# Issuing the stores of a gated activation from GpSimd's software queue instead of the scalar queue

## The chip, the cores and the metric

One core of one Trainium2 chip. The metric is the device time of one execution in microseconds (us). A time quoted is the median of the runs of a kernel. A ratio is the mean time of one kernel's fast runs over the mean of the other's fast runs of the same rounds, so it is not quite the ratio of the medians.

## The reference

```python
x = randn(8192, 8192) as float32
a, b = np.split(x, 2, axis=-1)
return a * (1 / (1 + np.exp(-b)))        # out: 8192 x 4096
```

It reads 268.4 MB and writes 134.2 MB, and computes one sigmoid and one product per output.

## The kernel before

The rows go through in 32 tiles of 256 rows, two rows per partition. There are two slots for the input (64 KB per partition each) and two for the output (32 KB per partition each). SP loads, ACT computes the sigmoid in place, DVE multiplies into the output slot, and ACT issues the store:

```python
xs = [pool.tile([P, R * n_cols], fp32, name=f"x_sb{k}") for k in range(SLOTS)]   # SLOTS = 2, R = 2
os = [pool.tile([P, R * half], fp32, name=f"o_sb{k}") for k in range(SLOTS)]
...
load = nc.sync.dma_start(out=xs[i % SLOTS], in_=x_t[i])
...
def store(cols):
    ins = nc.scalar.dma_start(out=out_t[i, :, cols], in_=os[i % SLOTS][:, cols])
...
    sig = nc.scalar.activation(out=b, in_=b, func=SIG)
    mul = nc.vector.tensor_mul(out=packed[:, r, c], in0=rows[:, r, 0, c], in1=b)
    ...
    by_sigmoid = i % 2 == 1 and len(parts) == 1
    implied(mul, *(s for s in old["stores"] if by_sigmoid or s not in freed))
    if by_sigmoid:
        for s in freed:
            tc.add_manual_dep(sig.ins, s.ins.name, DEP, reason="frees the output slot")
```

`implied` declares that a dependency needs no wait of its own. `freed` holds the stores of the tile two before, which free the output slot. In every second tile the sigmoid waits for them, in the others the product does. The first and the last tile are computed in four pieces; the last tile is also stored in four.

## Time and profile before

| | before |
|---|---|
| time, median | 933.88 us (933.03 to 934.08, 3 runs) |
| busy DVE, ACT | 30%, 24% of the span |
| DMA, 103 to 914 us | 434 GB/s, share 1.00 |
| a tile | one sigmoid every 29.0 us |
| a product, a sigmoid of a whole tile | 8.69 us, 7.03 us |

The share of the DMA engines is the time in which their packets were under way, averaged over the 16. (The profile counts a packet whole where it starts, so a short stretch can read a little over 1.00, as 0 to 22 us does with 1.02.) At 1.00, as here from 103 to 914 us, there is no time left in which a faster issue could start anything earlier. What bounds this kernel is therefore not read from the chain of waits (it gives DVE 15%), but from two things together: the share, and the *reserves*, that is, how long before it is needed each transfer is queued or done. The lines are in the prediction.

### The profile page before, as it was taken

Reading aid. Unit: us, or ns where it says so; the run is one execution under the profiler, and the core shown is the slowest. Engines: PE = TensorE matmul, PEld = TensorE weight load, DVE = VectorE, ACT = ScalarE, POOL = GpSimd, SP = SyncE. Lnnn points to the kernel's source line nnn. Section 1 sums busy time; section 2 is a strip of 40 time slices with the busy share of each in tenths; the row PEclk is TensorE's granted clock in tenths of the full one; section 3 lists DMA queues with packets and bytes.
Section 4 is the critical chain, followed back from the end, with each engine's and each line's share of the span. In section 5 each row is a group of like instructions: output and inputs, shape, how many; then the busy total and the mean of one; then the engine's idle time right before and its main releaser. Section 6 shows DMA issues by size and latency. Waiting matters only on the chain.

```text
span 931.7 us, 247 instructions
## 1 busy us (share of the span) xinstructions
DVE 278.7 (30%) x38; ACT 227.1 (24%) x39; POOL 0.2 (0%) x4
## 2 busy tenths in 40 slices
DVE  0333213333133331233312333123331233312333
ACT  1323330233311333113331133311333113332033
POOL 0000000000000000000000000000000000000000
DMA  9999999999999999999999999999999999999999
GB/s 405 428 450 428 422 456 405 450 428 428 450 418 438 428 436 442 428 428 450 447 408 428 442 459 428 413 460 411 450 428 425 453 408 447 428 428 450 425 430 405
DMA packets 9649, 402.67 MB, mean 432 GB/s; under 512 B 1072, under 2 KB 1072, under 8 KB 1072
## 3 DMA queue, kind: packets, MB, share of 16 engines
q1 hardware_dynamic: 4608, 268.44, 66.6%
q10 hardware_dynamic: 5040, 134.22, 33.4%
q14 instruction: 1, 0.01, 0.0%
HBM read 268.44 MB, written 134.22 MB: 432 GB/s over the span
## 4 chain that ended last, share of the span: by engine, by line
DMA 73%; DVE 15%; ACT 12%; issue 0%; ACTq 0%
DMA x_sb<-in_x_dram 73%; DVE o_sb L69 15%; ACT x_sb L68 12%; ACTq L62 0%; ACTq L68 0%
## 5 line engine op out<-in xcount | busy, mean ns | idle before, releaser
L69 DVE TENSOR_TENSOR o_sb<-x_sb 128x8192 f32<-128x8192 f32 (+1 forms) x38 | 278.7, 7344 | 647.1 <-ACT x_sb L68 647.1
L68 ACT ACTIVATE x_sb<-x_sb 128x8192 f32<-128x8192 f32 (+1 forms) x38 | 225.8, 5952 | 695.6 <-DMA x_sb<-in_x_dram 694.4
L68 ACT ACT_TABLE_LOAD x1 | 1.3, 1283 | 0.8 <-PEq L188 0.8
L188 POOL MEMSET const-bfloat16-1.0<- 128x1 bf16 x1 | 0.1, 102 | 0.0
L188 POOL MEMSET const-uint8-127<- 128x1 uint8 x1 | 0.1, 102 | 0.0
L188 POOL MEMSET const-float32-0.0<- 128x1 f32 x1 | 0.1, 99 | 0.2 <-issue 0.2
L188 POOL MEMSET const-float32-1.0<- 128x1 f32 x1 | 0.1, 99 | 0.0
## 6 DMA issues: line engine op xcount, KB each, us to landing
out_dram<-o_sb ACTq DMA_DIRECT2D x31, 4096.0 KB, 34.7
out_dram<-o_sb ACTq DMA_DIRECT2D x4, 1024.0 KB, 5.6
x_sb<-in_x_dram SPq DMA_DIRECT2D x32, 42.2
```

The lines of the kernel that those rows point to most:

```text
L68: sig = nc.scalar.activation(out=b, in_=b, func=SIG)
L69: mul = nc.vector.tensor_mul(out=packed[:, r, c], in0=rows[:, r, 0, c], in1=b)
L188: nc = _bacc.Bacc("TRN2", target_bir_lowering=False, num_devices=1)
```

## The change

The intent: take the stores off ACT's stream, so that a sigmoid never stands behind a store that waits for its product (in the kernel before this held ACT once, for 0.94 us, in the last tile), and let GpSimd, which was busy for 0.2 us there, issue them. The wait for the output slot goes to the sigmoid in every third tile instead of every second. The last two pieces stay on the scalar queue, presumably to end sooner, and the call that keeps the sigmoids in program order goes.

```diff
-        def store(cols):
-            ins = nc.scalar.dma_start(out=out_t[i, :, cols], in_=os[i % SLOTS][:, cols])
-            now["stores"].append(ins)
-
-        chunks = []
         for k, (r, c) in enumerate(parts):
 ...
-            by_sigmoid = i % 2 == 1 and len(parts) == 1
+            by_sigmoid = i % 3 == 2 and len(parts) == 1
 ...
-            tc.keep_in_program_order(sig)
             now["sigs"].append(sig)
             now["muls"].append(mul)
-            chunks.append(slice(r.start * half + c.start, r.start * half + c.stop))
-            if i == n_tiles - 1 and k > 0:
-                store(chunks[k - 1])
-        store(chunks[-1] if i == n_tiles - 1 else slice(0, R * half))
+            if i == n_tiles - 1:
+                cols = slice(r.start * half + c.start, r.start * half + c.stop)
+                queue = nc.scalar if k >= len(parts) - 2 else nc.gpsimd
+                store = queue.dma_start(out=out_t[i, :, cols], in_=os[i % SLOTS][:, cols])
+                now["stores"].append(store)
+        if i < n_tiles - 1:
+            now["stores"].append(nc.gpsimd.dma_start(out=out_t[i], in_=os[i % SLOTS]))
```

## The prediction

> **What bounds the kernel now.** I read the page first for the busy shares and the transfer rate, then the table of stretches for the rate in the steady part, then the timeline of one tile, then the waits, and the tile view for how long transfers take. The page:
>
> ```profile
> span 931.7 us, 247 instructions
> DVE 278.7 (30%) x38; ACT 227.1 (24%) x39; POOL 0.2 (0%) x4
> DMA  9999999999999999999999999999999999999999
> DMA packets 9649, 402.67 MB, mean 432 GB/s; under 512 B 1072, under 2 KB 1072, under 8 KB 1072
> q1 hardware_dynamic: 4608, 268.44, 66.6%
> q10 hardware_dynamic: 5040, 134.22, 33.4%
> DMA 73%; DVE 15%; ACT 12%; issue 0%; ACTq 0%
> ```
>
> No compute engine is busy for more than 30% of the span, and the 16 DMA engines are busy in every slice. The two queue lines say how transfers are cut: q1 holds the 32 loads, 4608/32 = 144 packets each, which I read as 128 data packets (one per partition, 8 MB/128 = 64 KB) and 16 completions. q10 holds 31 + 4 stores, 5040/35 = 144 each, so 32 KB per data packet in the 31 large ones. Reads are twice the writes, and the queues split the engines 2 to 1.
>
> The stretches (start:end and length, then busy time of DVE, ACT and POOL, clock, DMA share, GB/s):
>
> ```profile
> 0.00:22.00 22.00, 0.00 (x0) 1.33 (x2) 0.20 (x4) 1.00 1.02 429
> 22.00:45.00 23.00, 8.90 (x4) 7.47 (x5) 0.00 (x0) 1.00 0.98 410
> 103.00:914.00 811.00, 243.38 (x28) 196.75 (x28) 0.00 (x0) 1.00 1.00 434
> 925.00:928.00 3.00, 0.80 (x1) 0.00 (x0) 0.00 (x0) 1.00 1.00 421
> 928.00:930.00 2.00, 0.00 (x0) 0.00 (x0) 0.00 (x0) 1.00 1.00 422
> 930.00:931.70 1.70, 0.00 (x0) 0.00 (x0) 0.00 (x0) 1.00 0.49 207
> ```
>
> From 103 to 914 us the DMA engines are never idle and move 434 GB/s. All bytes at this rate are 402.67/434 = 927.8 us. So only about 4 us of the 931.7 us are not pure transfer at full rate: the start, a thin place at 22 to 45 us, and the last 1.7 us. The chain of waits puts 27% on DVE and ACT, but it follows one of the two slots alone: load 42.2, sigmoid 7.0, product 8.7, together 57.9 us per two tiles, while the other slot's load lies beside the compute. 57.9/2 = 29.0 us per tile is what 12.58 MB need at 434 GB/s. Shorter compute would only lengthen the time from issue to landing.
>
> The timeline around one tile, and the tile view of the output tensor, give the reserves:
>
> ```profile
> 582.58 58.54 SPq L50 DMA_DIRECT2D x_sb<-in_x_dram  x3
> 582.58 0.36 ACTq L62 DMA_DIRECT2D out_dram<-o_sb  x1
> 596.01 7.03 ACT L68 ACTIVATE x_sb<-x_sb 128x8192 f32<-128x8192 f32 x1 [22.18 <-DMA x_sb<-in_x_dram]
> 625.01 7.03 ACT L68 ACTIVATE x_sb<-x_sb 128x8192 f32<-128x8192 f32 x1 [21.97 <-DMA x_sb<-in_x_dram]
> 632.07 8.69 DVE L69 TENSOR_TENSOR o_sb<-x_sb 128x8192 f32<-128x8192 f32 x1 [20.31 <-ACT x_sb L68]
> ...
> DMA to landing us min/median/max: 5.4/34.7/34.9
> ```
>
> At 582.58 a product has ended; the load into its slot and its store are issued together. The load before it lands only at 596.0, so the load queue has its next work 596.0 - 582.6 = 13.4 us early. The store lands at 582.6 + 34.7 = 617.3; the sigmoid two tiles later, where odd tiles wait for the slot, starts at 625.0 (7.7 us in reserve), and its product, where even tiles wait, at 632.1 (14.8 us in reserve). The waits agree: no wait of ACT or DVE is put down to a store.
>
> ```profile
> ACT x_sb L68 <- DMA x_sb<-in_x_dram: 694.4, 32, 22.3
> DVE o_sb L69 <- ACT x_sb L68: 647.1, 33, 23.9
> ```
>
> [...]
>
> **The change, part by part.**
> - 33 of the 35 stores leave ACT: 33 x 0.36 = 12 us of ACT queue time go. ACT idles 22 us before each tile, so nothing of it is on the path.
> - The same 33 are written by GpSimd. [...] It falls into the 7.7 us reserve of each store; the engines meanwhile work on the load that was queued 13.4 us or more before. 0 us on the path. DVE is idle for 20.3 us after each product[...].
> - The instruction order has 10 sigmoids (tiles 2, 5, ..., 29) and 20 products that wait for a store, where before had 14 and 16. The waits are met 7.7 or 14.8 us early: 0 us.
> - GpSimd also waits for the store eight before, since eight semaphores go round: 8 x 29 = 232 us old. 0 us.
> - The last tile: the third sigmoid no longer stands behind a store (0.94 us of idle ACT). DVE sets that chain: its products ran from 916.65 to 925.80, and four of 2.29 us need 9.16 of these 9.15 us. Gain at most 0.2 us. The last store is issued at 925.8 by ACT as before, 1 MB at 434 GB/s is 2.4 us, but it shares the engines with what is queued, and the engines are full until 930. The end is the drain of a backlog whose bytes are the same. [...]
> - [...]
> [...] What can't be read from before is whether the software queue moves the same bytes as efficiently; for this I add 1.5 us. 933.9 + 2 = about 936 us.
>
> **The rivals.**
> - Smaller descriptors. If GpSimd cuts 32 KB rows into pieces of some 4 KB, each piece costs a fixed part. [...] For it: nothing in before fixes the cut. Against: 32 KB contiguous per partition leaves no need.
> - [...]
> - Another split between queues. Now 64 KB and 32 KB packets seem to alternate and both queues progress in the ratio of their work. If the software queue gets a larger share, stores land earlier and loads still are queued ahead: 934. If it gets a smaller one, stores land after more than 42 us and ACT begins to wait for stores on every third tile, on DVE after 49 us; the engines would still have the late stores to do while loads are held, so most of this is hidden: 935 to 945.
> - Faster. The floor is 927.8 us of transfer plus the start and the receipt of the last write, so about 930 by the span: 0.3% at best. Over 2% isn't there.
>
> **Range and chances.** The structure holds the time at the transfer bound, so nearly all weight is within 2% (915.2 to 952.6 us). 8 in 10: 932 to 950, skewed up because each uncertain term costs and none pays. Slower by over 2%[...]: 0.14. Faster by over 2%: 0.01. The rest, 0.85, is within.
>
> **What would show it right or wrong.** Right: the steady stretch at 433 to 434 GB/s with DMA share 1.00, 144 packets per store in the new queue, sigmoids 29.0 us apart, no ACT or DVE wait on a store, stores landing some 34 to 36 us after issue. Smaller descriptors: several times 144 packets and a lower rate at share 1.00. [...] Another split: store landings far from 34.7 us, and ACT or DVE waits on stores if late. Wrong altogether: POOL busy for many us per store, so that stores start late and the DMA share has holes; or a tail after the last product that is much longer than 6 us.

The small terms came to under 1 us with them; of those only the gain of at most 0.2 us in the last tile is left. With the 1.5 us, an allowance that comes from no trace, the sum was given as 2 us on top of 933.9, hence about 936 us.

What the packet records of the kernel before show: of the 144 packets of a transfer 128 carry data and 16 are of 4 bytes. A data packet of 64 KB took 2.418 us, one of 32 KB 1.213 us and one of 8 KB 0.309 us (medians): 1.205 us for each further 32 KB, so a fixed part of about 0.008 us per packet. The last landing came 0.32 us after the end of the last data packet. The queues do alternate: from the first to the last of the 128 data packets of a store, 96 packets of loads started (29 of the 30 large stores after the first). And in the changed kernel eight semaphores go round on GpSimd's stores; by the order of the records the store issued at 235.3 us follows the wait for the first, issued at 33.0 us, which is seven back.

## The result

The changed kernel takes 934.25 us (933.54 to 934.53, 6 runs), before in the same rounds 933.55 us (933.03 to 934.15, 6 runs): ratio 1.0006, 95% interval 0.9993 to 1.0019. The time is the same.

From the page of the changed kernel (the group line has the count, then busy us and the mean in ns, then the idle time before it):

```profile
q0 software_dynamic: 4752, 132.12, 32.8%
q10 hardware_dynamic: 288, 2.10, 0.5%
L82 POOL DMA_DIRECT2D out_dram<-o_sb x31 | 16.6, 536 | 886.5 <-DVE o_sb L66 886.5
```

The new queue q0 holds 33 stores in 4752 packets, 144 each as in the hardware queue: the 32 KB rows stayed whole. Its share per byte is that of q10 before (32.8% for 132.12 MB against 33.4% for 134.22 MB). GpSimd's instruction for a store takes 0.53 us.

Two of the same stretches as before:

```profile
22.00:45.00 23.00, 8.90 (x4) 7.20 (x4) 0.67 (x1) 1.00 0.95 388
103.00:914.00 811.00, 243.38 (x28) 196.81 (x28) 14.88 (x28) 1.00 1.00 434
```

The steady part is the same to the last digit: 434 GB/s, share 1.00. The thin place at 22 to 45 us reads 388 GB/s against 410 before, which is some 1.2 us of this execution (23 us x (1 - 388/410)). It doesn't follow the queue: two later runs read 399 GB/s there with the hardware queue (E3) and 410 with the software queue (E4).

One tile in the timeline, the waits, and the time to landing in the tile view of the output tensor:

```profile
583.77 58.33 SPq L52 DMA_DIRECT2D x_sb<-in_x_dram  x3
584.04 0.53 POOL L82 DMA_DIRECT2D out_dram<-o_sb  x1 [28.38 <-DVE o_sb L66]
597.04 7.03 ACT L65 ACTIVATE x_sb<-x_sb 128x8192 f32<-128x8192 f32 x1 [22.02 <-DMA x_sb<-in_x_dram]
626.00 7.03 ACT L65 ACTIVATE x_sb<-x_sb 128x8192 f32<-128x8192 f32 x1 [21.92 <-DMA x_sb<-in_x_dram]
...
DMA to landing us min/median/max: 5.2/34.6/35.4
```

```profile
POOL out_dram L82 <- DVE o_sb L66: 886.5, 31, 32.6
ACT x_sb L65 <- DMA x_sb<-in_x_dram: 695.8, 32, 22.5
DVE o_sb L66 <- ACT x_sb L65: 648.3, 32, 23.8
```

The load is issued at once when the product ends; the store starts on GpSimd 0.27 us after the load, where ACT started it with the load. It lands 34.6 us later, at 618.6, and the sigmoid two tiles on starts at 626.0: 7.4 us of reserve remain, against 7.7 before. (In this tile the product carries the wait. For the tile before it, whose sigmoid does, the same sum gives 597.04 - 555.13 - 34.6 = 7.3 us.) Sigmoids are 29.0 us apart as before. No wait of ACT or DVE is put down to a store, and GpSimd itself waits for nothing but products.

### The profile page after: what moved, and what is told of

Its sections match the earlier page's. It is cut to its first block, busy times and chain, and to the rows that moved or that the text cites. A ratio compares the mean times of both kernels' runs of the same rounds, so it can differ in the third digit from the quotient of the medians.

```text
span 933.1 us, 258 instructions
## 1 busy us (share of the span) xinstructions
DVE 278.6 (30%) x38; ACT 226.8 (24%) x39; POOL 17.9 (2%) x37
## 2 busy tenths in 40 slices
DMA packets 9649, 402.67 MB, mean 432 GB/s; under 512 B 1072, under 2 KB 1072, under 8 KB 1072
## 3 DMA queue, kind: packets, MB, share of 16 engines
q0 software_dynamic: 4752, 132.12, 32.8%
HBM read 268.44 MB, written 134.22 MB: 432 GB/s over the span
## 4 chain that ended last, share of the span: by engine, by line
DMA 73%; DVE 15%; ACT 12%; DVEq 0%; issue 0%; ACTq 0%
DMA x_sb<-in_x_dram 73%; DVE o_sb L66 15%; ACT x_sb L65 12%; DVEq L170 0%; ACTq L65 0%
## 5 line engine op out<-in xcount | busy, mean ns | idle before, releaser
L82 POOL DMA_DIRECT2D out_dram<-o_sb x31 | 16.6, 536 | 886.5 <-DVE o_sb L66 886.5
L79 POOL DMA_DIRECT2D out_dram<-o_sb x2 | 1.1, 531 | 18.6 <-DVE o_sb L66 18.6
## 6 DMA issues: line engine op xcount, KB each, us to landing
out_dram<-o_sb POOLq DMA_DIRECT2D x31, 4096.0 KB, 34.6
x_sb<-in_x_dram SPq DMA_DIRECT2D x32, 42.2
```

What stands on the lines that cost most here:

```text
L79: store = queue.dma_start(out=out_t[i, :, cols], in_=os[i % SLOTS][:, cols])
L82: now["stores"].append(nc.gpsimd.dma_start(out=out_t[i], in_=os[i % SLOTS]))
```

## The experiments

Twelve kernels ran, all with correct results. The theory: the time is that of the transfers, both kernels have the same transfers, and everything the change touches lies within the reserves. If so, two kinds of test must show it. More work inside the reserves must cost nothing, and where the reserves are taken away, the differences between the two kernels must come out. The rivals: the software queue is just as fast in itself; or a gain by one part hides a loss by another.

### E12: one part alone, the waits

```diff
-            by_sigmoid = i % 2 == 1 and len(parts) == 1
+            by_sigmoid = i % 3 == 2 and len(parts) == 1
```

> The kernel before with nothing changed but the waits for the output slot: on the sigmoid in tiles 2, 5, ..., 29 instead of 3, 5, ..., 29. One part of the change alone. Theory (the waits are met 7.7 or 14.8 us before they are asked): ratio 0.999 to 1.001 to before. If the changed kernel were the sum of a gain by one part and a loss by another, this would show over 0.2% either way.

933.39 us against 933.24: ratio 1.0000 (0.9988 to 1.0013). The waits alone move nothing, so the change isn't a gain by the waits hidden by a loss by the rest, or the reverse, beyond the 0.1% or so that the interval leaves.

### E3 and E4: more DVE work inside the reserve, and a DVE copy that holds GpSimd up

After each large product two useless copies run on DVE, over the input slot that is no longer needed, once in the kernel before and once in the changed one:

```diff
             now["muls"].append(mul)
+            if len(parts) == 1:
+                for _ in range(2):
+                    junk = nc.vector.tensor_copy(out=b, in_=rows[:, r, 0, c])
+                    implied(junk, *old["sigs"], *old["muls"], *old["loads"], *now["loads"])
```

> The kernel before with two useless copies on DVE after each large product, written over the x slot (results stay right). If the copies take 4.3 us each DVE has 8.6 us more per tile, 258 us in all, and the next load into the slot is issued 8.6 us later: its queue reserve sinks from 13.4 to about 5 us. Theory (transfer bound, reserves cover it): within 0.3% of before, 931 to 937 us, though the chain of waits gave DVE 15% of the span. Rival (the chain of waits is right that DVE is on the path): 8.6 us per tile pair per slot, so up to 130 us more. Control for the next run.

> The changed kernel with the same two copies right after each product[...]. Lock theory[...]: the POOL instruction of a store takes 4 to 9 us instead of 0.53, the store lands that much later counted from the end of its product; the sigmoid's wait on every third tile had 7.7 us in reserve, so the time is 933 to 945 us. No-lock theory: POOL stays at 0.53 us, landing as before. In both, the same within 2%; if slower by over 2% the lock also eats the reserves.

E3 took 933.94 us (ratio 1.0004, interval 0.9989 to 1.0019), E4 933.89 us (1.0003, 0.9988 to 1.0018). DVE's busy time rose from 279 to 544 us and nothing followed: the 13.4 us in which loads were queued ahead took up all of it. So DVE's 15% in the chain of waits was no cost. That chain must call something the reason for each wait, even where a transfer would only have waited longer in its queue: the loads, issued later, landed 33.3 us after issue instead of 42.2 (medians).

The timeline of E4:

```profile
499.11 4.43 DVE L78 COPY x_sb<-x_sb 128x8192 f32<-128x8192 f32 x1
...
524.75 8.89 DVE L78 COPY x_sb<-x_sb 128x8192 f32<-128x8192 f32 x2
525.01 4.29 POOL L86 DMA_DIRECT2D out_dram<-o_sb  x1 [25.81 <-DVE o_sb L66]
```

The first line shows a single copy: 4.43 us. The pair at 524.75 has its first copy end near 529.18, and the POOL instruction ends at 529.30. GpSimd's instruction for a store, 0.53 us in the changed kernel, takes 4.29 us here (the median of the 31), until 0.12 us after the first copy; the second copy, which ran on to 533.64, held it no longer. So the lock theory is right in what it expects of the time: a copy on DVE held GpSimd's store instruction up. What ties the two no run shows. The stores landed 36.8 us after their issue, against 31.4 in E3; that was still in time. In the changed kernel as it stands, DVE idles when GpSimd issues the large stores (from 583.77, where a product ends and GpSimd's instruction follows at 584.04, to the next product). The product itself did not hold GpSimd up: its instructions for the first two stores of the last tile took 0.53 us each, at 920.54 and 922.75, while DVE was at the products of the next pieces (917.95 to 926.85).

### E1 and E2: the reserve taken away

One output slot instead of two, in the kernel before (E1) and the changed one (E2). Every product now waits for the store of the tile before it.

```diff
-    os = [pool.tile([P, R * half], fp32, name=f"o_sb{k}") for k in range(SLOTS)]
+    os = [pool.tile([P, R * half], fp32, name="o_sb0")] * SLOTS
```

(The lists of freed stores follow: each product waits for the last tile's store, the sigmoids for none.)

> The kernel before with one output slot instead of two, so that every product waits for the store of the tile before it and the time from the end of a product to the landing of its store comes onto the path. Theory (the store's path is hidden in both kernels by 7 to 15 us of reserve): with the reserve gone the engines run dry during each product; a tile takes one product (8.7 us) plus the landing of a store that shares the engines with one load (4.2 + 8.4 MB at 434 GB/s = 29 us, and about 2 us of issue and receipt), so some 39.5 us and 1250 to 1290 us in all. Rival (the output slots are not what holds things together, the transfer bound alone counts): stays within 2% of 934 us. This is the control for the next run.

> The changed kernel with one output slot. Theory that the software queue is slower per store but hidden in the changed kernel: POOL starts 0.29 us after the product where ACT starts 0.02 us after, and then takes 0.53 us against 0.36, so 0.3 to 0.8 us more per tile on the path, 31 tiles: 9 to 25 us (0.7 to 2%) slower than the same kernel with the hardware queue. Rival (nothing differs at all, the paths are equally fast): within 0.3% of it. Rival (the software queue delivers fewer bytes per us, hidden somewhere): more than 3% slower.

E1 took 1306.13 us (ratio to before 1.3996), a little over the range expected (a store took 32.7 us to land, not 31; the 2 us for issue and receipt were an estimate, and a store alone, in E11, took 11.1 us, of which 0.84 us pass before its first data packet and 9.7 are its bytes at 434 GB/s); E2 took 1298.06 us (1.3920). The first part of the expectation holds: without reserve the kernel is 40% slower and the DMA share from 103 to 800 us falls to 0.73. The second part is a miss: the software queue was not 9 to 25 us slower but 8 us *faster*, though GpSimd starts later, and none of the three expectations gave that. The difference is 0.6%, small, but the runs do not overlap (1305.06 to 1309.14 and 1297.21 to 1303.84 us, 4 each). The waits of DVE, E1 first:

```profile
DVE o_sb L70 <- DMA out_dram<-o_sb: 996.5, 31, 33.8
```

```profile
DVE o_sb L67 <- DMA out_dram<-o_sb: 988.9, 31, 34.3
```

(996.5 - 988.9)/31 = about 0.25 us less per tile between the end of a product and the landing of its store. So either the software path is faster in itself, or the sharing with the load beside it changed. E11 was made to tell these apart.

### E11: the disputed cost by itself

From the changed kernel: each load waits for the store of the tile before, so that nothing lies beside a store; stores of odd tiles go through GpSimd, those of even ones through ACT.

```diff
+        for s in last_stores[(i + 1) % SLOTS]:
+            tc.add_manual_dep(load.ins, s.ins.name, DEP, reason="nothing beside a store")
 ...
-            now["stores"].append(nc.gpsimd.dma_start(out=out_t[i], in_=os[i % SLOTS]))
+            now["stores"].append((nc.gpsimd if i % 2 else nc.scalar).dma_start(out=out_t[i], in_=os[i % SLOTS]))
```

> The disputed cost by itself: every load waits for the store of the tile before, so nothing lies beside a store, and stores of odd tiles go through GpSimd, those of even tiles through ACT, in one execution. A tile takes a load (8.4 MB, about 22 us as the first one took), 15.8 us of compute and a store (9.7 us at 434 GB/s and some 2 us more): about 49.5 us, 1560 to 1620 us in all. What counts is the time from the end of the product to the next load's issue, odd against even tiles. Theory of a slower software path: odd tiles 0.3 to 0.9 us longer. Theory after the one-slot runs (software landing is no later, though it starts later): within 0.2 us or shorter on odd tiles; then the gain there is in the path of the store itself, else it came from the sharing with a load.

1557.69 us in one run, just under the range expected. The chain of waits (start, length, what), first an even tile, then an odd one:

```profile
515.35 8.70 DVE o_sb L68
524.05 0.02 issue
524.07 11.10 DMA out_dram<-o_sb
535.17 0.02 SPq L52
...
564.26 8.70 DVE o_sb L68
572.97 0.28 issue
573.25 11.35 DMA out_dram<-o_sb
584.60 0.02 issue
```

From the end of the product to the landing: 535.17 - 524.05 = 11.12 us by ACT, 584.60 - 572.96 = 11.64 us by GpSimd. By itself the software path is 0.5 us slower per 4 MB store: 0.27 us until it starts and 0.25 us more to landing. Where these 0.25 us lie, the stretches right after the two issues show:

```profile
524.07:524.85 0.78, 0.00 (x0) 0.00 (x0) 0.00 (x0) 1.00 0.00 0
573.25:574.30 1.05, 0.00 (x0) 0.00 (x0) 0.53 (x1) 1.00 0.00 0
```

Nothing moves yet in either. By the packet records of the trace the first data packet starts 0.84 us after the issue by ACT (median of 16 stores, 0.84 to 0.88) and 1.10 us by GpSimd (15 stores, 1.09 to 1.23). From there to the landing both take 10.26 us, so once a store moves, the two queues are equally fast, though odd tiles also use the other output slot.

So the slower-path theory is right about the path, and the 0.25 us that E2 gained must have come where a store and a load share the engines. The packet records fit: the store's first data packet starts 6.9 us after its issue in E2 and 4.6 us in E1 (medians), so the two mix differently. Whether this is because the load's issue comes 0.27 us first in E2, or by another difference between the two kernels, is left open; no run varied the order by itself. In the changed kernel both effects are inside the 7.4 us of reserve and show nowhere.

### E5 to E8: small pieces, the prediction's first rival

Output slots with a gap of 16 bytes after every 4 KB (C = 1024), or after every 1 KB (C = 256), so that a store can't move whole rows. From the kernel before (the product and the last pieces are re-cut in the same way):

```diff
-    os = [pool.tile([P, R * half], fp32, name=f"o_sb{k}") for k in range(SLOTS)]
+    C = 1024
+    os = [pool.tile([P, R * half // C, C + 4], fp32, name=f"o_sb{k}") for k in range(SLOTS)]
 ...
+        cut = os[i % SLOTS][:, :, 0:C]
+        out_v = out_t[i].rearrange("p (q c) -> p q c", c=C)
 ...
-            ins = nc.scalar.dma_start(out=out_t[i, :, cols], in_=os[i % SLOTS][:, cols])
+            ins = nc.scalar.dma_start(out=out_v[:, cols], in_=cut[:, cols])
```

> The kernel before with output slots whose 4 KB pieces are 16 bytes apart, so that a store can't go as 32 KB rows but as 8 pieces of 4 KB per partition: 1024 data packets instead of 128. It sets what small pieces cost on the hardware queue. Theory of the prediction's first rival (a 4 KB piece costs a fixed part): 10 to 25 us more than before, 944 to 958 us. Second possibility: [...]stores land late and ACT and DVE wait for them: landing over 42 us, time 945 to 990. If neither: 934.

> The changed kernel with the same 4 KB pieces. If GpSimd's writing time goes with the number of descriptors (0.53 us for 144), it is 3.8 us for 1040, hidden in the reserve: equal to the hardware queue's 4 KB run within 1%. If it has a large fixed part and a small one per descriptor, about 1 us. [...]

> The same with 1 KB pieces on the hardware queue: 4096 data packets per store. Fixed cost per piece four times that of 4 KB[...]. 960 to 1100 us; ACT's issue of a store (0.36 us) may grow to several us.

> The same with 1 KB pieces on the software queue. Proportional writing: 15 us of POOL per store, below the 29 us period, but more than the 7.7 us reserve, so the time would be up to 3% above the hardware queue's 1 KB run; with POOL over 29 us per store it would become the bound. Small cost per descriptor: equal within 1%.

(The fixed part per piece is the 0.008 us per packet beside the prediction. How a store of small packets would share the engines with a load, and a cost of reading descriptors, no run shows. "Writing" in E6 and E8 is the time of GpSimd's store instruction; what it does in that time the traces do not show.)

| | 4 KB pieces | 1 KB pieces |
|---|---|---|
| hardware queue | E5 976.87 us, ratio 1.0466 | E7 1025.61 us, 1.0985 |
| software queue | E6 1017.38 us, ratio 1.0899 | E8 1046.41 us, 1.1211 |

The stretch from 103 to 800 us of E5, then of E6:

```profile
103.00:800.00 697.00, 199.93 (x23) 165.82 (x24) 0.00 (x0) 1.00 1.00 413
```

```profile
103.00:800.00 697.00, 195.14 (x23) 156.79 (x23) 18.42 (x22) 1.00 0.96 397
```

E5 costs 43 us, where 10 to 25 were expected of small pieces, and its engines are never idle: they are busy and move less, 413 GB/s (402.67/413 = 975 us). Stores now land 45.3 us after issue (median), so the reserve is gone. The waits of ACT in E5:

```profile
ACT x_sb L71 <- DMA out_dram<-o_sb: 446.9, 14, 32.2
```

All 14 sigmoids that carry the wait for the slot now wait for a store, up to 32.2 us. Still the engines are full. What is not separated is the size of the pieces from where they start: the gap of 16 bytes shifts each piece in its partition, and no run kept 4 KB pieces without the gap.

E6 is 40 us (4%) slower than E5, more than any of its expectations allowed, and GpSimd's instruction isn't to blame: 0.84 us of POOL per store of 1024 pieces, against 0.53 us for 128 rows, and 1.64 us for 4096 pieces in E8, so a large fixed part and a small one per piece. What differs is the share, 0.96. Busy engines move 397/0.96 = 413 GB/s, the same as in E5. So the engines ran *dry*; where, the timeline and stretches of E6 show:

```profile
471.94 13.95 ACT L68 ACTIVATE x_sb<-x_sb 128x8192 f32<-128x8192 f32 x2 [61.48 <-DMA out_dram<-o_sb]
472.00:500.00 28.00, 17.29 (x2) 13.89 (x2) 1.68 (x2) 1.00 0.79 322
```

A sigmoid waits 61 us for a store. When it may run, the next one runs right behind it: both inputs had landed and both slots stood still. No load can be issued until a sigmoid and a product are through, and in these 28 us the engines have a share of 0.79. The wait sits on the sigmoid in every third tile; so the suspect is the second part of the change, not the queue.

The packets of E8 and E7 held a surprise. E8's software queue first, then E7's hardware queue, then two stores of E7 in the timeline:

```profile
q0 software_dynamic: 32784, 132.12, 34.2%
```

```profile
q10 hardware_dynamic: 131632, 134.22, 37.0%
486.35 0.54 ACTq L65 DMA_DIRECT2D out_dram<-o_sb  x1
502.78 31.89 ACTq L65 DMA_DIRECT2D out_dram<-o_sb  x1
```

The software queue has as many packets for 1 KB pieces as for 4 KB ones (32784 in E6 too): it joined them to 4 KB. The hardware queue made one packet per piece, and at every second large store (15 of 31) the issue held ACT for 29.6 to 32.0 us; the next sigmoid stood behind it. The other 16 took 0.54 to 0.63 us (against 0.36 us for 128 rows of 32 KB), the first of all among them, which had no store ahead of it. So it isn't the number of pieces alone that holds ACT: the held ones were issued while the store before was still under way (the one at 486.35 landed 53.6 us later, at 540.0). What exactly they wait for no run shows. E8's time against E7's doesn't say which queue is better for 1 KB, because E8 also carries the waits of every third tile; no version of it without them ran. Only the rate of busy engines can be compared: 386 GB/s at share 0.96 in E8, so about 402, against 394 at 1.00 in E7 (103 to 800 us).

### E9 and E10: which part of the change loses the 40 us

E5 with the waits of every third tile, E6 with those of every second: the single line shown under E12, applied in either direction.

> The hardware queue's 4 KB run with one edit: the wait for the output slot is on the sigmoid in every third tile, as in the changed kernel, instead of every second. It is to say where the 40 us between the two 4 KB runs (977 and 1017 us) come from. Wait theory (the distribution of waits makes the engines run dry once stores land late, share 0.96 instead of 1.00): this run rises to 1010 to 1020 us with share 0.96. Queue theory (the software queue itself loses the time): it stays at 974 to 980 us.

> The software queue's 4 KB run with the wait on the sigmoid in every second tile, as before. Wait theory: falls from 1017 to 972 to 982 us with DMA share 1.00 and 413 GB/s. Queue theory: stays at 1010 to 1020 us. If half of each, some 995 in both.

| 4 KB pieces | sigmoid waits in every second tile | in every third |
|---|---|---|
| hardware queue | E5 976.87 us, share 1.00 | E9 1012.20 us, share 0.96 |
| software queue | E10 981.64 us, share 1.00 | E6 1017.38 us, share 0.96 |

The stretch from 103 to 800 us of E9, then of E10:

```profile
103.00:800.00 697.00, 194.64 (x23) 155.67 (x23) 0.00 (x0) 1.00 0.96 399
103.00:800.00 697.00, 199.92 (x23) 165.62 (x24) 19.24 (x23) 1.00 1.00 413
```

The waits cost 35 us in either queue (1012.20 - 976.87, and 1017.38 - 981.64), the software queue, with the parts of the change that go with it, 5 us under either distribution of waits. The two add. The 5 us are not a cost per tile: E10 moves 413 GB/s at share 1.00 in the steady stretch, as E5 does, and its last product ends at 964.4 us, E5's at 965.0. But E10's span ends 15.1 us after that product and E5's 10.6 us, and E6 and E9 differ in the same way (15.2 and 10.6). So nearly all of it is paid once, in the last stores; why they take longer no run shows. So the line of the waits that was worth 0.0% in E12 is worth 3.6% where stores land late. Every second tile is always the same slot; every third falls on the two slots by turns. That this is why both slots get stuck fits the timeline of E6, but was only argued.

## Why the prediction was right

- *Transfer bound.* Shown: 434 GB/s at share 1.00 in both kernels, and 8.9 us more of DVE work per tile changed nothing (E3, E4).
- *12 us of ACT queue time off the path.* Right: they are gone and the time is the same.
- *The stores through GpSimd, hidden.* Hidden: the reserve before the sigmoid shrank from 7.7 to 7.4 us. The extra time per store that the step put down rested on figures that no trace here shows. Measured alone (E11) it is 0.5 us: the first data packet is 0.26 us later (1.10 against 0.84), and 0.27 us pass from the end of the product to GpSimd's start.
- *Waits met early.* Right: E12, ratio 1.0000.
- *Semaphores that go round.* Right that they cost nothing: no wait of GpSimd is put down to a store. (By the order of the records in the trace the wait goes back seven stores, some 203 us, not eight.)
- *Last tile.* The four products took 8.90 us instead of 9.15, a gain of 0.25 us against at most 0.2 predicted. That four products need 9.16 us was a wrong sum, since back to back they take less than four times one: the first tile's four took 8.90 us in the kernel before already. The gain shows nowhere in the time, as the step said; from the end of the last product to the end of the span the profile has 6.25 us, before 5.9.
- *144 packets per store in the new queue.* Right.
- *The 1.5 us added for an unknown efficiency.* The largest term of the sum, an allowance and not measured, and it was not needed. With it the forecast was about 2 us more than before; measured were 0.7 us by the medians, and the interval (-0.07% to +0.19%) can't tell this from zero.
- *Rival of small descriptors.* It didn't occur. Its size was not shown by any trace; E5 measured 43 us with stores of 4 KB pieces.
- *Second rival.* The sign that it was to show, a steady share under 1.00, was not seen: the share is 1.00.
- *Rival of another split.* It didn't occur with 32 KB packets. The statement that of late stores "most of this is hidden" holds with the waits of every second tile, where the engines stay full, and fails with those of every third, which this change brings: 35 us (E9).

## What to carry to other kernels

Before moving an issue from one engine to another, read the reserves: how long before it is needed each transfer is queued or landed. While they held here, the queue, the engine that issues and the place of a wait made no difference (ratio 1.0006 for the change, 1.0000 in E12), and neither did 8.9 us more compute per tile (1.0004 and 1.0003 in E3 and E4). Once they were gone, the place of the wait mattered more than the queue (35 us against 5 in E5, E6, E9 and E10), so try the distribution of the waits by itself. That the better one won because it leaves one slot able to move is argued, not shown.
